# Hybrid decoder step on one core: the FFN's list of waiting pair work goes on across tiles, and sums of weights are made up to three units ahead

## The chip, the core and the metric

One Trainium2 chip, one core of it. The metric is device time in microseconds (us) of one launch. Engines: PE (TensorE, matrix products; PEld are its weight loads), DVE (VectorE), ACT (ScalarE), POOL (GpSimd), SP (SyncE, which here only issues loads).

## What is computed

A two-layer decoder trunk for 512 prompt tokens and 8 sample tokens, width 1024, float32. Each layer adds half a SwiGLU FFN, a mixing stage and another half FFN:

```python
def swiglu_ffn(x, wg, wu, wd):
    return (jax.nn.silu(x @ wg) * (x @ wu)) @ wd

x = x + 0.5 * swiglu_ffn(rms_norm(x, g1), wg1, wu1, wd1)
x = x + mix(rms_norm(x, gm))       # retention, sliding window attention, conv
x = x + 0.5 * swiglu_ffn(rms_norm(x, g2), wg2, wu2, wd2)
```

The FFN's hidden width is 2816. So there are four FFN blocks in the program, and the change lies in these alone.

## The kernel before

**Layout.** The activations x lie transposed: 8 blocks of 128 features by 520 columns (512 + 8), worked on as two halves of 260. Float32 products are made of a rounded high part and a low remainder of each factor. For each weight, ACT casts the high part (L290) and DVE subtracts to get the low part (L296); three matmuls then make one product (`mm3`, L342; `product`, L334).

**Weights.** They come in the order of use as 318 chunks of 128 x 1024 floats (512 KB) into a ring of four places, loaded by SP's queue (`load`, L238 to L245). A place is loaded anew when the last low split of its chunk is done. `ahead` (L303) is called at the start of each unit of weights: it issues the casts of units up to six slots ahead (a plain chunk is two slots, a product one), then the low splits, and then sums for coming units.

**Tiles.** A hidden tile is 128 of the 2816 hidden features: 22 tiles, numbered 0 to 21, each with a gate half (t) and an up half (u). The down projection runs in three steps: after tiles 0 to 8 step 0 uses tiles 0 to 7; after tiles 9 to 16 step 1 uses tiles 8 to 15; after tiles 17 to 21 step 2 uses the rest.

**Seven products.** The tiles 5, 6, 7, 9, 10, 11, 13, 14, 15, 17, 18, 20 and 21 ("paired") and down steps 0 and 1 take 2 x 2 block products with seven products instead of eight: a11, s1, s2, a12, s3, s4, a22 (`seven`, L523). s1, s2 and s4 need sums of weights, made by `sums` (L247) on DVE: s1 at L258, s2 at L260 and L261, s4 at L263. The chunk with a22 is released by a22's low split. In `seven`, ACT copies c11 to c22 (L528) ahead of product s2. On the side of the activations, sums of four blocks are needed too: `sum_parts` (L476) makes four sums on DVE (L461 to L464), two casts on ACT (L480) and two low splits on DVE (L484). `pair_blocks` (L499) puts three casts (L509) and three splits (L512) before it.

A plain tile (`hidden`, L439) has 16 weight tiles on PE, eight for the gate half and eight for the up half; after the first half DVE scales the gate half out of PE's result (L448), at the end the up half (L454).

**The list.** What follows a tile is put into a list of generators, `waiting`: first `gated` (L426), the gating u*silu(t) (L429 and L431 for paired tiles, silu at L434 on ACT, product L436 on DVE); then, for tiles with an odd number in groups 0 and 1, `pair_blocks`. `advance` (L412) does one step of the first generator in the list. It is called at every second weight tile of a plain tile and between the products of `seven`. `flush` (L420) does all that is left; `ffn` (L581) calls it at the end of each hidden tile, before the new work is put in, and at the start of each down step.

Each engine does its instructions in the order in which they are issued; where one waits, all behind it wait.

Of the kernel before, what the change touches and what calls it, by code (L numbers as in the profile page):

```python
# [23 lines left out]
PAIRED = (5, 6, 7, 9, 10, 11, 13, 14, 15, 17, 18, 20, 21)  # L24


GROUPS = ((0, 8, True), (8, 16, True), (16, 22, False))
# [91 lines left out]
def ffn_tiles(first, gate, up):  # L119


    return [(o, k) for k in range(KD) for o in (gate, up)] if first else [(o, k) for o in (gate, up) for k in range(KD)]
# [14 lines left out]
def step_kernel(ctx: ExitStack, tc: tile.TileContext, io: dict):  # L137
# [46 lines left out]
    def v2(t):  # L184
        return t.rearrange("p (a b) -> p a b", a=2)

    def unit(dt=F32):
        return units.tile([128, UNIT], dt, tag="m", name="m")
# [6 lines left out]
    def wt(name, n=NT, dt=F32, bufs=None):  # L195
        return work.tile([128, n], dt, tag="t", name=name)

    def ptile():
        return psum.tile([128, 2, 512], F32, tag="o", name="o")
# [4 lines left out]
    seq, slot = [], [0]  # L204
# [14 lines left out]
    chunk = [0]  # L219
# [16 lines left out]
    at, nxt, loaded, pending = [0, 0], [0], [0], []  # L236

    def load(dma=True):  # L238

        while loaded[0] < NCH and (loaded[0] < RAW or loaded[0] - RAW in done):  # L240
            i = loaded[0]
            loaded[0] += 1
            raw[i] = wraw.tile([128, CT * 128], F32, tag="w", name="w")
            if dma:
                nc.sync.dma_start(raw[i], io["w"][i])  # L245

    def sums(u):  # L247

        if u >= len(seq) or u in ready:
            return  # L250
        ready.add(u)
        name, i = seq[u]
        if name == "chunk":
            return
        load()
        (a21, a11), (a22, a12) = ((raw[j][:, :PC], raw[j][:, PC:]) for j in (i, i + 1))
        if name == "s1":
            nc.vector.tensor_add(Rd[:, 0, :PC], a21, a22)  # L258
        elif name == "s2":
            nc.vector.tensor_sub(a21, a21, a11)  # L260
            nc.vector.tensor_add(Rd[:, 1, :PC], a21, a22)  # L261
        elif name == "s4":
            nc.vector.tensor_sub(Rd[:, 0, :PC], a12, Rd[:, 1, :PC])  # L263
# [18 lines left out]
    def split_hi():  # L282

        u = nxt[0]
        if u < len(seq):
            nxt[0] += 1
            load()
            sums(u)
            spl[u] = parts_of(u)
            nc.scalar.copy(spl[u][0], source(u))  # L290
            pending.append(u)

    def split_lo(n=9):
        for u in pending[:n]:
            h, lo = spl[u]
            nc.vector.tensor_sub(lo, source(u), h.bitcast(F32))  # L296
            name, i = seq[u]
            if name in ("chunk", "s3", "a22"):
                done.add(i + (name == "a22"))
                load()  # L300
        del pending[:n]

    def ahead(u):  # L303

        old = len(pending)
        while nxt[0] < len(seq) and slot[nxt[0] + 1] - slot[u] <= 6:
            split_hi()
        if seq[u][0] == "chunk":
            split_lo()
        else:  # L310
            split_lo(old)
            sums(nxt[0])
            sums(nxt[0] + 1)

    def next_tile(look=True):
        u, c = at
        if c == 0 and look:
            ahead(u)
        at[:] = (u, c + 1) if c + 1 < CT else (u + 1, 0)
        s = slice(c * 128, (c + 1) * 128)  # L320
        return spl[u][0][:, s], spl[u][1][:, s]
# [17 lines left out]
    def mm3(o, w, vh, vl, first, last):  # L339
        for i, (a, b) in enumerate(((w[0], vl), (w[0], vh), (w[1], vh))):  # L340
            for s in range(2):
                nc.tensor.matmul(  # L342
                    o[:, s, :HN], lhsT=a, rhs=b[:, s * HN : (s + 1) * HN],
                    start=first and i == 0, stop=last and i == 2,
                )
# [20 lines left out]
    def run(parts):  # L366
        for _ in parts:
            pass
# [43 lines left out]
    waiting = []  # L412

    def advance():
        while waiting:
            try:
                next(waiting[0])
                return True
            except StopIteration:
                del waiting[0]  # L420

    def flush():
        while advance():
            pass
# [14 lines left out]
    def hidden(norm, first):  # L439

        og, ou = ptile(), ptile()
        for i, (o, k) in enumerate(ffn_tiles(first, og, ou)):
            mm3(o, next_tile(), xh[:, k], xl[:, k], k == 0, k == KD - 1)
            if i % 2:
                advance()
            if i + 1 == KD and not first:
                t = wt("t")
                nc.vector.tensor_mul(v2(t), og[:, :, :HN], v2(R))  # L448
        if first:
            run(norm)  # L450
            t = wt("t")
            nc.vector.tensor_mul(v2(t), og[:, :, :HN], v2(R))
        u = wt("u")
        nc.vector.tensor_mul(v2(u), ou[:, :, :HN], v2(R))  # L454
        return t, u, None

    def sums4(u, w):


        (b11, b12), (b21, b22) = ((z[:, :HN], z[:, HN:]) for z in (u, w))  # L460
        nc.vector.tensor_sub(b22, b12, b22)  # L461
        nc.vector.tensor_sub(b12, b12, b11)  # L462
        nc.vector.tensor_sub(b11, b11, b22)
        nc.vector.tensor_sub(b21, b21, b11)  # L464
        return u, w
# [4 lines left out]
    def meet(b, t):  # L470
        return {n: (b, t)[i][c] for n, (i, c) in MEET.items()}

    def halves(h, lo):
        return [tuple(z[:, i * HN : (i + 1) * HN] for z in (h, lo)) for i in range(4)]

    def sum_parts(th, tl, u, w):  # L476
        sums4(u, w)
        yield
        for i, src in enumerate((u, w)):
            nc.scalar.copy(th[:, i * NT : (i + 1) * NT], src)  # L480
        yield
        for i, src in enumerate((u, w)):
            c = slice(i * NT, (i + 1) * NT)
            nc.vector.tensor_sub(tl[:, c], src, th[:, c].bitcast(F32))  # L484
        yield
# [13 lines left out]
    def pair_blocks(u, w, spare, hs):  # L499

        if not spare:
            z = [unit(F32R) for _ in range(3)]
            spare += [z[i // 4][:, i % 4 * HN : (i % 4 + 1) * HN] for i in range(12)]
        th, tl = unit(F32R), unit(F32R)
        b = [(spare.pop(0), spare.pop(0)) for _ in range(3)]
        hs.append(meet(b, halves(th, tl)))
        src = u[:, :HN], w[:, :HN], w[:, HN:]
        for (h, _), a in zip(b, src):
            nc.scalar.copy(h, a)  # L509
        yield  # L510
        for (h, lo), a in zip(b, src):
            nc.vector.tensor_sub(lo, a, h.bitcast(F32))  # L512
        yield from sum_parts(th, tl, u, w)

    def two_parts(u, hs):
# [65 lines left out]
    def ffn(l, name, norm, after):  # L581
        hs, even, spare, xs = {n: [] for n in range(len(GROUPS))}, None, [], []
        for step, n in ffn_steps():
            if step == "hidden":
                g = next(i for i, (a, b, _) in enumerate(GROUPS) if a <= n < b)
                t, u, v = pair_hidden(xs) if n in PAIRED else hidden(norm, n == 0)
                flush()
                waiting.append(gated(t, u, v))
                if GROUPS[g][2] and n % 2:
                    waiting.append(pair_blocks(even, u, spare, hs[g]))  # L590
                elif GROUPS[g][2] or n == GROUPS[g][0]:
                    even = u
                else:
                    waiting.append(two_parts(u, hs[g]))
                waiting.extend(input_sums(l, name, j, xs) for j in {0: (0,), 1: (1, 2), 2: (3,)}.get(n, ()))
                continue
            flush()
            if GROUPS[n][2]:
                for m in range(0, KD, 2):
                    pair_down(m, hs[n])  # L600

                if not GROUPS[n + 1][2]:
                    waiting.append(two_parts(even, hs[n + 1]))
                continue
            if n == len(GROUPS) - 1 and name == "ffn1_norm":
                load_mix_constants()
            for m in range(KD):
                o = ptile()
                for f, h in enumerate(hs[n]):
                    mm3(o, next_tile(), *h, f == 0, f == len(hs[n]) - 1)  # L610
                nc.vector.scalar_tensor_tensor(
                    v2(x[:, m]), o[:, :, :HN], 0.5, v2(x[:, m]), op0=ALU.mult, op1=ALU.add
                )
                if n == len(GROUPS) - 1:
                    run(after(m))
# [818 lines left out]
```

## Time and profile before

| | us |
|---|---|
| three runs | 1906.8, 1906.71, 1905.59 |
| median | 1906.71 |
| the profiled execution | 1903.99 |
| its span | 1902.2 |
| its mean granted PE clock | 0.989 of full speed |

All times inside the prediction are of the profiled execution, counted from the start of its span. In rows of a timeline the columns are start, duration, engine, line, operation, out<-in and count; the bracket holds the idle time of the engine ahead of it and what ended it. Instructions of one line that follow each other are one row, with a count. Rows of waits give the total, how many times and the longest. Windows give the busy time of each engine in a stretch and PE's granted clock.

### The profile page before, as it was taken

What the parts mean: (1) busy time and instruction counts of PE and PEld (TensorE: products, weight loads), DVE (VectorE), ACT (ScalarE), POOL (GpSimd) and SP (SyncE); (2) the same over time, 40 slices, a digit from 0 to 9 for tenths busy, and PEclk for the clock granted to TensorE, in tenths of its full rate; (3) what the DMA queues carried; (4) which work ended last, traced back from release to release, by engine and by line L of the source; (5) the groups of instructions that cost most, each with busy time, mean ns of one, the idle gap of its engine ahead of it and who ended that gap; (6) DMA issues with size and microseconds to landing.
All of it is one profiled execution on the core that took longest, in us unless ns stands there. A gap on an engine that the chain in (4) does not pass through costs nothing.

```text
span 1902.2 us, 37220 instructions
## 1 busy us (share of the span) xinstructions
PE 1845.5 (97%) x15182; PEld 1821.8 (96%) x15182; DVE 1552.9 (82%) x2587; ACT 1051.3 (55%) x2052; POOL 23.3 (1%) x52
## 2 busy tenths in 40 slices
PE   8999999999999999999999999999998999999999
PEld 8999999999989999999999999999998999999999
DVE  8988888688667989888779888876886579889984
ACT  6655646533765656645555556565237556466452
POOL 0000000000100000000000000000000000000000
PEclk9999999999999999999999999999999999999999
DMA  5233224433312233323323232434333132333332
GB/s 182 79 100 112 90 89 127 129 104 115 117 43 92 78 90 100 102 88 107 116 80 100 87 92 89 124 114 125 101 113 105 45 100 68 95 108 100 92 96 90
DMA packets 54173, 189.37 MB, mean 100 GB/s; under 512 B 6273, under 2 KB 7153, under 8 KB 54001
## 3 DMA queue, kind: packets, MB, share of 16 engines
q1 hardware_dynamic: 50784, 177.35, 30.8%
q0 software_dynamic: 3072, 9.53, 1.5%
q8 instruction: 119, 1.95, 0.4%
q14 instruction: 54, 0.43, 0.1%
q10 hardware_dynamic: 144, 0.11, 0.0%
HBM read 179.50 MB, written 7.45 MB: 98 GB/s over the span
## 4 chain that ended last, share of the span: by engine, by line
PE 68%; DVE 20%; ACT 5%; issue 4%; DMA 3%; DVEq 0%; ACTq 0%; POOL 0%; POOLq 0%
PE o L342 37%; PE o L334 29%; DVE wl L296 4%; DVE wh L296 3%; DMA w<-in_w 2%; DVE m L484 2%; DVE u L436 1%; DVE m L512 1%; DVE u L431 1%; DVE w L260 1%; DVE t L431 1%; DVE t L429 1%; PE o L361 1%; ACT wh L290 1%; DVE u L462 1%
## 5 line engine op out<-in xcount | busy, mean ns | idle before, releaser
L342 PE MATMUL o<-xl,wh 128*128 128x260 f32 x1920 | 389.8, 284 | 6.5 <-DVE xl L387 6.0
L342 PE MATMUL o<-xh,wl 128*128 128x260 f32 x1920 | 387.6, 284 | 0.9 <-DVE wl L296 0.9
L342 PE MATMUL o<-xh,wh 128*128 128x260 f32 x1920 | 387.4, 283 | 0.0
L334 PE MATMUL o<-m,wh 128*128 128x260 f32 x2592 | 352.9, 286 | 16.8 <-ACT o L528 15.5
L290 ACT CAST wh<-w 128x1024 fp32r<-128x1024 f32 (+1 forms) x318 | 261.4, 822 | 193.3 <-PE o L342 134.9
L334 PE MATMUL o<-m,wl 128*128 128x260 f32 x2592 | 352.4, 285 | 16.2 <-ACT o L528 15.1
L334 PEld LDWEIGHTS o<-m,wh 128*128 128x128 f32 x2592 | 330.3, 191 | 20.9 <-ACT o L528 18.5
L334 PEld LDWEIGHTS o<-m,wl 128*128 128x128 f32 x2592 | 329.5, 190 | 20.0 <-ACT o L528 17.9
L342 PEld LDWEIGHTS o<-xl,wh 128*128 128x128 f32 x1920 | 297.4, 189 | 7.8 <-ACT wh L355 5.9
L342 PEld LDWEIGHTS o<-xh,wl 128*128 128x128 f32 x1920 | 297.1, 189 | 1.1 <-DVE wl L296 1.1
L342 PEld LDWEIGHTS o<-xh,wh 128*128 128x128 f32 x1920 | 296.6, 189 | 0.0
L296 DVE TENSOR_TENSOR wl<-w,wh 128x1024 fp32r<-128x1024 f32 x150 | 183.3, 1222 | 45.3 <-ACT wh L290 40.0
L342 PE MATMUL o<-m,wh 128*128 128x260 f32 x1024 | 164.5, 282 | 1.7 <-DVE m L520 1.7
L342 PEld LDWEIGHTS o<-m,wh 128*128 128x128 f32 x1024 | 140.0, 188 | 2.5 <-DVE m L520 2.5
L296 DVE TENSOR_TENSOR wh<-w,wh 128x512 fp32r<-128x512 f32 x168 | 115.1, 685 | 8.8 <-ACT wh L290 8.8
L296 DVE TENSOR_TENSOR wl<-w,wl 128x512 fp32r<-128x512 f32 x168 | 115.1, 685 | 8.7 <-ACT wl L290 8.7
L290 ACT CAST wl<-w 128x512 fp32r<-128x512 f32 x168 | 104.3, 621 | 30.0 <-PE o L334 16.1
L334 PE MATMUL o<-xh,wl 128*128 128x260 f32 x624 | 115.8, 283 | 0.0
L334 PE MATMUL o<-xh,wh 128*128 128x260 f32 x624 | 115.5, 282 | 0.0
L290 ACT CAST wl<-Rd 128x512 fp32r<-128x512 f32 x126 | 78.5, 623 | 59.6 <-PE o L334 27.8
L290 ACT CAST wh<-Rd 128x512 fp32r<-128x512 f32 x126 | 78.5, 623 | 57.5 <-PE o L334 26.3
L342 PE MATMUL o<-m,wl 128*128 128x260 f32 x512 | 102.7, 282 | 0.0
(219 smaller groups left out, 2674.7 us busy)
## 6 DMA issues: line engine op xcount, KB each, us to landing
w<-in_w SPq DMA_DIRECT2D x318, 512.0 KB, 3.6
out_y<-x SPq DMA_DIRECT2D x8, 260.0 KB, 2.0
m<-in_cm POOLq DMA_DIRECT2D x4, 512.0 KB, 4.2
m<-in_s_ret SPq DMA_DIRECT2D x4, 512.0 KB, 5.7
m<-sc POOLq DMA_DIRECT2D x8, 256.0 KB, 4.4
out_o_rets<-m POOLq DMA_DIRECT2D x4, 512.0 KB, 3.5
x<-in_x SPq DMA_DIRECT2D x3, 520.0 KB, 6.8
w<-in_w SPq DMA_DIRECT2D x4, 256.0 KB, 4.9
```

The costliest lines, as they stand in the source:

```text
L260: nc.vector.tensor_sub(a21, a21, a11)
L290: nc.scalar.copy(spl[u][0], source(u))
L296: nc.vector.tensor_sub(lo, source(u), h.bitcast(F32))
L334: nc.tensor.matmul(o, lhsT=a[:, s], rhs=b, start=first and j == 0 and i == 0, stop=j == JP - 1 and i == 2, skip_group_check=True,)
L342: nc.tensor.matmul(o[:, s, :HN], lhsT=a, rhs=b[:, s * HN : (s + 1) * HN], start=first and i == 0, stop=last and i == 2,)
L361: nc.tensor.matmul(o[:, s, :HN], lhsT=w, rhs=v[:, s * HN : (s + 1) * HN], start=i == 0, stop=i == len(parts) - 1,)
L429: nc.vector.tensor_add(d[:, HN:], d[:, HN:], v)
L431: nc.vector.tensor_mul(d, d, R)
L436: nc.vector.tensor_mul(u, u, t)
L462: nc.vector.tensor_sub(b12, b12, b11)
L484: nc.vector.tensor_sub(tl[:, c], src, th[:, c].bitcast(F32))
L512: nc.vector.tensor_sub(lo, a, h.bitcast(F32))
```

## The change

Four things change, all in the order in which the FFN's side work is issued.

1. `ahead` makes the sums of up to three coming units, where it made those of two. It stops at a unit whose chunks are not yet loading, and at an s1 while an s4 still waits for its low split.
2. `ffn` empties the list at the end of tiles 0 to 4 only. From tile 5 on the work of a tile stays in the list and goes on in the next tile, in order. At down steps 0 and 1 the list is emptied but for its last item, the gating of the plain tile just computed (8 or 16), which goes on in the down step.
3. `hidden` takes a step of the list at each weight tile, not only every second, while more than two items wait.
4. `sum_parts` gets an empty step behind its four sums, and `pair_blocks` one ahead of them: the same work in more steps.

```diff
@@ ahead
             split_lo(old)
-            sums(nxt[0])
-            sums(nxt[0] + 1)
+            for v in range(nxt[0], min(nxt[0] + 3, len(seq))):
+
+                load()
+                if seq[v][0] != "chunk" and seq[v][1] + 1 >= loaded[0]:
+                    break
+                if seq[v][0] == "s1" and any(seq[p][0] == "s4" for p in pending):
+                    break
+                sums(v)
@@ hidden
-            if i % 2:
+            if i % 2 or len(waiting) > 2:
                 advance()
@@ sum_parts
         sums4(u, w)
         yield
+        yield
         for i, src in enumerate((u, w)):
@@ pair_blocks
             nc.vector.tensor_sub(lo, a, h.bitcast(F32))
+        yield
         yield from sum_parts(th, tl, u, w)
@@ ffn
                 t, u, v = pair_hidden(xs) if n in PAIRED else hidden(norm, n == 0)
-                flush()
+                if n < PAIRED[0]:
+                    flush()
                 waiting.append(gated(t, u, v))
...
+            rest = [waiting.pop()] if GROUPS[n][2] else []
             flush()
+            waiting.extend(rest)
             if GROUPS[n][2]:
```

The same instructions are issued on each engine, and PE's order is the same; DVE's and ACT's orders differ. The lines of the new kernel lie 6 to 8 below those of the old (L436 is L442, L448 is L454, L454 is L460, L461 to L464 are L467 to L470, L484 is L491, L429 is L435, L431 is L437, L512 is L519); L258 to L296 keep their numbers.

Three places on DVE, in the first FFN block. First the passage from the last paired tile (7) to the plain tile 8, before:

```order
L484 TENSOR_TENSOR m<-u,m 128x520 x2
L296 TENSOR_TENSOR wh<-w,wh 128x512
L429 TENSOR_TENSOR t<-t,v 128x260
L429 TENSOR_TENSOR u<-u,v 128x260
L431 TENSOR_TENSOR t<-t,R 128x520
L431 TENSOR_TENSOR u<-u,R 128x520
L296 TENSOR_TENSOR wl<-Rd,wl 128x512
L296 TENSOR_TENSOR wh<-w,wh 128x512
L436 TENSOR_TENSOR u<-u,t 128x520
L296 TENSOR_TENSOR wl<-w,wh 128x1024
L258 TENSOR_TENSOR Rd<-w 128x512
```

The same place in the new kernel (an L296 of 128x512 is the low split of a product's weights, from Rd where these are a sum; one of 128x1024 that of a plain chunk):

```order
L296 TENSOR_TENSOR wl<-Rd,wl 128x512
L491 TENSOR_TENSOR m<-u,m 128x520 x2
L296 TENSOR_TENSOR wh<-w,wh 128x512
L435 TENSOR_TENSOR t<-t,v 128x260
L435 TENSOR_TENSOR u<-u,v 128x260
L437 TENSOR_TENSOR t<-t,R 128x520
L437 TENSOR_TENSOR u<-u,R 128x520
L258 TENSOR_TENSOR Rd<-w 128x512
L296 TENSOR_TENSOR wl<-w,wh 128x1024
L442 TENSOR_TENSOR u<-u,t 128x520
```

The four gating rows (L429 and L431, now L435 and L437) stand behind the two splits of s4 and a22, and the sum L258 of the next pair stands ahead of the plain chunk's split and of the product L436 (L442).

Next the start of down step 0 on DVE, from the last of the four sums to the sum s1 of the next unit, before:

```order
L464 TENSOR_TENSOR u<-u 128x260
L484 TENSOR_TENSOR m<-u,m 128x520 x2
L454 TENSOR_TENSOR u<-o,R 128x520
L436 TENSOR_TENSOR u<-u,t 128x520
L263 TENSOR_TENSOR Rd<-w,Rd 128x512
L296 TENSOR_TENSOR wl<-w,wl 128x512
L296 TENSOR_TENSOR wh<-Rd,wh 128x512
L258 TENSOR_TENSOR Rd<-w 128x512
```

The same place in the new kernel, down to the product of tile 8's gating:

```order
L470 TENSOR_TENSOR u<-u 128x260
L460 TENSOR_TENSOR u<-o,R 128x520
L491 TENSOR_TENSOR m<-u,m 128x520 x2
L263 TENSOR_TENSOR Rd<-w,Rd 128x512
L296 TENSOR_TENSOR wl<-w,wl 128x512
L296 TENSOR_TENSOR wh<-Rd,wh 128x512
L258 TENSOR_TENSOR Rd<-w 128x512
L260 TENSOR_TENSOR w<-w 128x512
L261 TENSOR_TENSOR Rd<-w 128x512
L442 TENSOR_TENSOR u<-u,t 128x520
```

The scaling L454 (L460) goes ahead of the splits of the activations, and the product L436 (L442) goes behind the sum s4 and the next sums.

Last, tile 4 on DVE, from the splits of three blocks to the sum s4, before:

```order
L512 TENSOR_TENSOR m<-u,m 128x260 x3
L461 TENSOR_TENSOR u<-u 128x260
L462 TENSOR_TENSOR u<-u 128x260
L463 TENSOR_TENSOR u<-u 128x260
L464 TENSOR_TENSOR u<-u 128x260
L448 TENSOR_TENSOR t<-o,R 128x520
L260 TENSOR_TENSOR w<-w 128x512
L261 TENSOR_TENSOR Rd<-w 128x512
L296 TENSOR_TENSOR wh<-Rd,wh 128x512
L296 TENSOR_TENSOR wl<-w,wl 128x512
L484 TENSOR_TENSOR m<-u,m 128x520 x2
L454 TENSOR_TENSOR u<-o,R 128x520
```

The same place in the new kernel:

```order
L519 TENSOR_TENSOR m<-u,m 128x260 x3
L454 TENSOR_TENSOR t<-o,R 128x520
L260 TENSOR_TENSOR w<-w 128x512
L261 TENSOR_TENSOR Rd<-w 128x512
L296 TENSOR_TENSOR wh<-Rd,wh 128x512
L296 TENSOR_TENSOR wl<-w,wl 128x512
L467 TENSOR_TENSOR u<-u 128x260
L468 TENSOR_TENSOR u<-u 128x260
L469 TENSOR_TENSOR u<-u 128x260
L470 TENSOR_TENSOR u<-u 128x260
L491 TENSOR_TENSOR m<-u,m 128x520 x2
L460 TENSOR_TENSOR u<-o,R 128x520
```

The four sums go behind the scaling of the gate half (L448, now L454), the sum s2 and two splits.

## The prediction

> **What bounds the kernel now.** I read the page's summary first, then the waits of the matmul engine, then those places engine by engine.
>
> ```profile
> PE 1845.5 (97%) x15182; PEld 1821.8 (96%) x15182; DVE 1552.9 (82%) x2587; ACT 1051.3 (55%) x2052; POOL 23.3 (1%) x52
> ```
>
> PE is busy 97% of the span, so the time can fall only where PE stands still. The waits of PE, longest total first (us in total, times, longest):
>
> ```profile
> PE o L334 <- ACT o L528: 30.6, 13, 3.0
> ```
>
> The copy L528 (c22 <- c11, ahead of product s2 of a seven-product tile) holds PE for 30.6 us. Twelve of the thirteen waits are long, three in each of the four FFN blocks: at the start of down step 0 (place 1), at hidden tile 13 (place 2) and at the start of down step 1 (place 3). These are the three of the first block, each stretch from the first product of the tile to the end of the wait (PE, PEld, DVE, ACT, POOL busy, granted clock, DMA share):
>
> ```profile
> 109.39:115.36 5.97, 3.04 (x26) 2.84 (x24) 5.45 (x11) 3.15 (x7) 0.00 (x0) 1.00 0.01 3
> 195.36:200.59 5.23, 3.05 (x26) 2.84 (x24) 4.76 (x10) 2.62 (x6) 0.00 (x0) 1.00 0.00 0
> 240.22:246.30 6.08, 3.15 (x27) 2.87 (x25) 5.56 (x11) 3.15 (x7) 0.00 (x0) 1.00 0.01 3
> ```
>
> DVE is busy for nine tenths of each stretch while PE does 3.0 us of work in 5.2 to 6.1: DVE ends last here. Place 1 on PE, ACT and DVE, in time:
>
> ```profile
> 115.36 0.39 PE L334 MATMUL o<-m,wl 128*128 128x260 f32 x1 [2.93 <-ACT o L528]
> ...
> 114.42 0.62 ACT L290 CAST wh<-Rd 128x512 fp32r<-128x512 f32 x1 [1.82 <-DVE Rd L263]
> 114.94 0.37 ACT L528 COPY o<-o 128x260 f32<-128x260 f32 x1
> ...
> 110.40 0.43 DVE L464 TENSOR_TENSOR u<-u 128x260 f32<-128x260 f32 x1
> 111.05 1.31 DVE L484 TENSOR_TENSOR m<-u,m 128x520 fp32r<-128x520 f32 x2 [0.23 <-ACT m L480]
> 112.28 0.69 DVE L454 TENSOR_TENSOR u<-o,R 128x520 f32<-128x520 f32 x1
> 113.08 0.70 DVE L436 TENSOR_TENSOR u<-u,t 128x520 f32<-128x520 f32 x1
> 113.70 0.68 DVE L263 TENSOR_TENSOR Rd<-w,Rd 128x512 f32<-128x512 f32 x1
> ```
>
> PE waits for L528; on ACT's queue L528 stands behind the cast of the sum s4, which waits for L263; on DVE's queue L263 stands behind L484, L454 and L436, none of which it needs. Place 2 has the same shape, without L436 ahead of the sum:
>
> ```profile
> 197.04 1.31 DVE L484 TENSOR_TENSOR m<-u,m 128x520 fp32r<-128x520 f32 x2 [0.23 <-ACT m L480]
> 198.27 0.69 DVE L454 TENSOR_TENSOR u<-o,R 128x520 f32<-128x520 f32 x1
> 198.88 0.68 DVE L263 TENSOR_TENSOR Rd<-w,Rd 128x512 f32<-128x512 f32 x1
> ```
>
> Why DVE comes late to place 1 is seen one tile earlier on DVE, at the passage from the last seven-product tile (7) to the plain tile 8:
>
> ```profile
> 91.09 0.42 DVE L429 TENSOR_TENSOR t<-t,v 128x260 f32<-128x260 f32 x1
> ...
> 93.00 0.68 DVE L296 TENSOR_TENSOR wl<-Rd,wl 128x512 fp32r<-128x512 f32 x1
> 93.60 0.69 DVE L296 TENSOR_TENSOR wh<-w,wh 128x512 fp32r<-128x512 f32 x1
> 94.20 0.69 DVE L436 TENSOR_TENSOR u<-u,t 128x520 f32<-128x520 f32 x1
> 94.81 1.22 DVE L296 TENSOR_TENSOR wl<-w,wh 128x1024 fp32r<-128x1024 f32 x1
> 98.23 0.69 DVE L258 TENSOR_TENSOR Rd<-w 128x512 f32<-128x512 f32 x1 [2.20 <-DMA w<-in_w]
> 98.84 1.22 DVE L296 TENSOR_TENSOR wl<-w,wh 128x1024 fp32r<-128x1024 f32 x1
> 99.97 0.69 DVE L260 TENSOR_TENSOR w<-w 128x512 f32<-128x512 f32 x1
> ```
>
> ```profile
> 94.31 3.80 DMA w<-in_w
> ```
>
> The split at 93.60 is the last use of a raw chunk (a22); the load into that place takes 3.80 us; L258, the next pair's sum s1, waits 2.20 us for it; and from there to L263 at 113.70 the chain of waits names DVE, with short casts of ACT between, and never PE. In all, DVE waits for loads at L258:
>
> ```profile
> DVE Rd L258 <- DMA w<-in_w: 20.8, 10, 2.3
> ```
>
> So the end of place 1 is set by the a22 split one tile earlier, plus the load, plus the row of DVE work behind it.
>
> **The change, part by part.** It adds and removes no instruction; PE's order stays. Only DVE and ACT rows move. All lines below are those of the kernel before.
>
> *At tiles 7, 11 and 15 the gating goes behind the splits.* The list is no longer emptied at the tile's end, so L429 twice and L431 twice now stand behind the splits of s4 and a22: from 91.09 to 93.00, 1.91 us of DVE work. The a22 split, and with it the load, can start up to x = 1.91 us earlier. Lower bound x = 0 (the split waits for something else). The load may also take longer, as it starts closer to the one before. Two loads 2 us apart:
>
> ```profile
> L245 SPq DMA_DIRECT2D w<-in_w x2: 327/328/328, 124.4 to 126.4; - x2
> ...
> DMA to landing us min/median/max: 3.6/4.0/4.5
> ```
>
> Against 3.80 that is up to 0.7 more. Here the load before is the one that the s3 split releases: 3.1 us earlier now (91.09 to 94.20, the rows behind each split), 2.4 us then, since one split and two L484 still lie between and the gating doesn't (0.6 + 1.2 + 0.6, an estimate from the spacings above). That is a third of the way from 3.1 to 2.0, so I take 0.2 of the 0.7: x = 1.7.
>
> *L258 goes ahead of plain work.* Looking three units ahead puts L258 in front of tile 8's first split (94.81; the next such one, 98.84 to 99.97, holds DVE 1.13) and of L436 (94.20 to 94.81, 0.61), which filled the time until the landing. So 1.74 us that lay beside the load now lies behind it. DVE's wait at L258 hardly shrinks, and tile 8's first split comes late for PE. I price that second effect at nothing: the split would end at 98.23 - 1.7 + 0.61 + 1.22 = 98.4 and not at 96.0, so PE loses at most 2.3 us there, even if it used the split at once; place 1 ends by DVE's row, 2.93 us behind PE, and what PE loses in tile 8 it waits less at place 1. If DVE were not last there, it would cost up to 2.3 us a place, 28 in all.
>
> [...]
>
> *At places 1 and 3* L436 goes behind L263, and L454 goes ahead of L484, where it fills the idle 0.23. L436 costs 113.70 - 113.08 = 0.62, the gap ahead of it 113.08 - 112.28 = 0.80 less the usual 0.61 (198.88 - 198.27), 0.19; with the 0.23 that is 1.04 less ahead of L263. *At place 2* L263 goes ahead of the two L484: 198.27 - 197.04 = 1.23, and the 0.23 ahead of them, 1.46.
>
> So L528 comes earlier, at places 1 and 3 by x - 1.74 + 1.04 = x - 0.70, at place 2 by x - 1.74 + 1.46 = x - 0.28. A block gains 3x - 1.68; with x = 1.7 that is 3.42, four blocks 13.7. The places add up, since DVE waits for PE again between them. No place has its wait used up: 1.0 of 2.9 at places 1 and 3, 1.4 of some 2.2 at place 2.
>
> *A loss at tile 4 to 5.* The extra step in the list puts the four sums L461 to L464 behind L448, L260, L261 and two splits. L448 needs the first half of tile 4 on PE. Second block, DVE, ACT, PE:
>
> ```profile
> 640.52 0.43 DVE L461 TENSOR_TENSOR u<-u 128x260 f32<-128x260 f32 x1
> ...
> 642.26 0.69 DVE L448 TENSOR_TENSOR t<-o,R 128x520 f32<-128x520 f32 x1
> ...
> 646.23 1.30 DVE L484 TENSOR_TENSOR m<-u,m 128x520 fp32r<-128x520 f32 x2
> ...
> 648.06 0.68 DVE L263 TENSOR_TENSOR Rd<-w,Rd 128x512 f32<-128x512 f32 x1
> ...
> 649.35 0.37 ACT L528 COPY o<-o 128x260 f32<-128x260 f32 x1
> ...
> 641.16 0.40 PE L342 MATMUL o<-xl,wh 128*128 128x260 f32 x2
> ...
> 649.80 1.44 PE L334 MATMUL o<-m,wl 128*128 128x260 f32 x10
> ```
>
> Today the L461 group fills DVE's time until PE is at its half (641.16). Now L448 stands there and waits, as it does in another tile, for the half plus 0.19 us (311.51 - 311.32):
>
> ```profile
> 311.51 0.70 DVE L448 TENSOR_TENSOR t<-o,R 128x520 f32<-128x520 f32 x1 [0.62 <-PE o L342]
> ...
> 311.32 0.40 PE L342 MATMUL o<-xl,wh 128*128 128x260 f32 x2
> ```
>
> L448 then starts at 641.16 + 0.19 = 641.35, not 642.26, and DVE is idle for 0.8 us ahead of it. The rows behind come 0.91 earlier, up to L484's old slot (646.23 - 0.91 = 645.32). There the four sums stand now: three spacings of 0.47 and, from L464 to L484 through the casts L480, 0.65 (111.05 - 110.40), 2.05 in all. L484 comes at 647.37, 1.14 later, and with it L263 and L528. L528 ended at 649.72 and PE was ready at 649.80: a new wait of 1.06 us in blocks two to four. In the first block PE waits there already, and by the same walk L263 moves by 0.78: 0.8 more.
>
> ```profile
> 69.74 1.71 PE L334 MATMUL o<-m,wh 128*128 128x260 f32 x12 [0.17 <-ACT o L528]
> ```
>
> Sum 3 x 1.06 + 0.8 = 4.0. Bounds: 0 (the first half of tile 4 is done earlier against DVE than in this run) and 4 x 1.14 + the 0.4 that a further wait for the casts adds, 5.
>
> *The rest* (the list running on in tiles 5 to 7, 9 to 11, 13 to 15 and 17 to 21; the last gating kept for the down step, where DVE has its own slack beside four tiles of products) I cost at nothing: PE shows no wait there. Cover gone, it would be L436's 0.6 us a place.
>
> **Sum.** 1903.99 (span 1902.2 and 1.8 around it) - 13.7 + 4.0 = 1894.3. The median of the three runs, 1906.71, lies 2.7 above the profiled run; the same is added: **1897.0**. Own range: x = 1.91 without the loss gives -16.2, 1890.5; x = 1.2 (the landing's whole 0.7 lost) with it gives -3.7, 1903.
>
> **Rivals.**
> - *The waits at L528 vanish* (DVE gets ahead for good, as its idle time before L258 is used): -30.6 + 4.0, 1880 (1876 without the loss, 1889 if a third of them stays). For: 10 waits of DVE there are 20.8 us. Against: L258 still waits for its load. Chance 0.12.
> - *No change.* The load is slower by what it starts earlier, and x stays near 0.89, at which 12x - 6.7 only pays the 4.0: 1903 to 1910, that is x from 1.2 to 0.6. For: the 4.5 us landing, 0.7 over 3.80; a pause of DVE ahead of the a22 split that takes another 0.3. Chance 0.12.
> - *Slower: the landing gates plain work.* If the a22 split is not earlier (x = 0: its cast on ACT or the products release it, not DVE's row), L258 with its wait stands in front of tile 8's split for nothing. Places 1 and 3 lose 0.70, place 2 0.28: 4 x 1.68 + 4.0 = +10.7, 1917. It decides below x = 0.89. Worse, a wait of 2.93 + 0.70 = 3.6 us nears the one after which PE's clock falls. After a wait of 4.63 us in the mixing stage it was halved:
>
> ```profile
> 522.85:527.48 4.63, 0.00 (x1) 0.00 (x1) 3.82 (x8) 4.50 (x9) 0.00 (x0) 0.92 0.00 0
> 527.48:531.00 3.52, 3.52 (x16) 2.68 (x17) 3.45 (x7) 3.46 (x8) 0.00 (x0) 0.50 0.02 5
> ```
>
> Half speed for 3.52 us loses 1.8 us a time, at eight places 14 more: 1917 to 1932. Against: DVE's rows from 91.09 to 94.20 stand back to back, so DVE's row does hold the split, as far as the rows show. Chance 0.12.
>
> [...]
>
> **How the numbers follow.** Forecast 0.64, the three rivals 0.12 each. No change can be told within 0.2%, 3.8 us: 1902.9 to 1910.5. The forecast's own range and the first rival lie below that, the second rival within, the third above: 0.76, 0.12, 0.12. The range takes the forecast whole, most of the no-change case and the upper half of the bigger gain: 1884 to 1908, leaving out the slower case and half of the first rival, 0.18.
>
> **What would show it.** Right: the waits for L528 still twelve long ones, places 1 and 3 near 1.9 and place 2 near 0.8 us, some 22 in all with the new ones (30.6 - 13.7 + 4.0 = 20.9); L258's DVE wait near 2.2 at the last paired tile, now ahead of the plain tile's split; a short PE wait for that split; a new wait of about 1 us for L528 in tile 5. Wrong: long waits gone or as long as before; a22's split at tile 7 not earlier against PE; the clock below 1.00 behind place 1 or 3; a long PE wait inside a down step, where I priced the kept gating at nothing.

## The result and the profile after

| | before | after |
|---|---|---|
| median, us | 1906.76 (1905.59 to 1913.0) | 1889.13 (1888.96 to 1890.91) |
| profiled execution, us | 1903.99 | 1888.96 |
| its span | 1902.2 | 1886.9 |
| its PE busy time | 1845.5 | 1835.9 |
| its mean granted clock | 0.989 | 0.995 |

The ratio is 0.9912, with an interval of 0.9896 to 0.9929: 17.6 us faster, where the prediction said 9.7 (1906.71 to 1897.0) with a range of 1884 to 1908. The direction and the range hold; more than half of the size comes from where the prediction had put nothing, PE's clock. The page after, then the waits of PE (L536 is the copy L528 of before):

```profile
PE 1835.9 (97%) x15182; PEld 1812.8 (96%) x15182; DVE 1558.1 (83%) x2587; ACT 1050.7 (56%) x2052; POOL 23.3 (1%) x52
```

```profile
PE o L340 <- ACT o L536: 18.1, 16, 1.6
PE o L348 <- DVE wl L296: 8.8, 13, 1.6
```

The waits for the copy fell by 12.5 us, from 30.6; waits for the plain tile's split rose by 7.9, of which 7.2 are twelve new waits at tiles 8, 12 and 16 (the one wait of before, 0.9, lies in the mixing stage). PE's time outside its busy time is 1902.2 - 1845.5 = 56.7 before and 1886.9 - 1835.9 = 51.0 after, 5.7 less. The other 9.6 of the span's 15.3 us are busy time, with the same 15182 matmuls: PE ran faster. The clock shows it. The first 3.4 us behind each long wait before (PE, PEld, DVE, ACT, POOL busy, granted clock, DMA share, GB/s):

```profile
115.36:118.76 3.40, 3.40 (x28) 3.40 (x29) 3.33 (x6) 2.08 (x5) 0.00 (x0) 1.00 0.57 170
...
246.30:249.70 3.40, 3.40 (x18) 3.40 (x19) 3.33 (x6) 1.86 (x4) 0.00 (x0) 0.58 0.69 180
...
825.73:829.13 3.40, 3.40 (x21) 3.40 (x22) 3.33 (x6) 1.91 (x4) 0.00 (x0) 0.71 0.65 171
1058.03:1061.43 3.40, 3.40 (x20) 3.40 (x21) 3.33 (x6) 1.91 (x4) 0.00 (x0) 0.68 0.67 180
1144.40:1147.80 3.40, 3.40 (x16) 3.40 (x17) 3.33 (x6) 2.29 (x6) 0.00 (x0) 0.53 0.61 165
1191.55:1194.95 3.40, 3.40 (x18) 3.40 (x19) 3.33 (x6) 1.90 (x4) 0.00 (x0) 0.62 0.66 186
1641.70:1645.10 3.40, 3.40 (x20) 3.40 (x21) 3.33 (x6) 1.91 (x4) 0.00 (x0) 0.68 0.63 178
```

Behind six of the twelve waits PE ran for part of the time at half speed, 16 to 21 matmuls in 3.40 us instead of 28. Six times 3.40 us times what is missing to 1.00 (2.20 in sum) is 7.5 us lost inside these windows. The half-speed stretches run on past them: in the trace's record of the clock each of the six lasts 3.41 us at 0.50, so six lose up to 10.2 us, which covers the 9.6. After the change all twelve windows show 1.00, such as these:

```profile
114.84:118.24 3.40, 3.40 (x28) 3.40 (x29) 3.30 (x6) 2.61 (x6) 0.00 (x0) 1.00 0.52 154
...
1133.55:1136.95 3.40, 3.40 (x28) 3.40 (x29) 3.30 (x6) 2.77 (x6) 0.00 (x0) 1.00 0.49 130
```

Now the passage from tile 7 to tile 8 on DVE (L437 is L431, L442 is L436), with PE's first matmuls of tile 8:

```profile
92.54 0.69 DVE L296 TENSOR_TENSOR wh<-w,wh 128x512 fp32r<-128x512 f32 x1
...
94.43 0.69 DVE L437 TENSOR_TENSOR u<-u,R 128x520 f32<-128x520 f32 x1
97.08 0.69 DVE L258 TENSOR_TENSOR Rd<-w 128x512 f32<-128x512 f32 x1 [1.96 <-DMA w<-in_w]
97.69 1.22 DVE L296 TENSOR_TENSOR wl<-w,wh 128x1024 fp32r<-128x1024 f32 x1
98.83 0.69 DVE L442 TENSOR_TENSOR u<-u,t 128x520 f32<-128x520 f32 x1
...
97.90 0.40 PE L348 MATMUL o<-xl,wh 128*128 128x260 f32 x2
...
98.97 0.51 PE L348 MATMUL o<-xh,wl 128*128 128x260 f32 x2 [0.43 <-DVE wl L296]
```

The a22 split starts 1.06 us earlier (93.60 to 92.54), not 1.91, counted from the start of the span, in which PE has lost 0.8 us more by then, in tile 5; L258 still waits about 2 us; the plain split and L442 stand behind it, and PE waits for that split. The rest of place 1:

```profile
113.18 0.68 DVE L263 TENSOR_TENSOR Rd<-w,Rd 128x512 f32<-128x512 f32 x1
...
114.84 0.63 PE L340 MATMUL o<-m,wl 128*128 128x260 f32 x3 [1.52 <-ACT o L536]
```

From L258 to L263 it is 16.10 us here, against 15.47 before (98.23 to 113.70): 0.63 more, where the prediction had 1.74 - 1.04 = 0.70. And the forecast loss at tile 4 to 5 is there. L454 (L448 of before) waits for PE in tile 4, and PE waits for the copy in tile 5:

```profile
60.89 0.70 DVE L454 TENSOR_TENSOR t<-o,R 128x520 f32<-128x520 f32 x1 [0.96 <-PE o L348]
...
70.47 0.74 PE L340 MATMUL o<-m,wh 128*128 128x260 f32 x4 [0.97 <-ACT o L536]
```

### The profile page after: what moved, and what is told of

Same layout as the page of the kernel before. It is cut to its first block, busy times and chain, and to the rows that moved or that the text cites. A ratio compares the mean times of both kernels' runs of the same rounds, so it can differ in the third digit from the quotient of the medians.

```text
span 1886.9 us, 37178 instructions
## 1 busy us (share of the span) xinstructions
PE 1835.9 (97%) x15182; PEld 1812.8 (96%) x15182; DVE 1558.1 (83%) x2587; ACT 1050.7 (56%) x2052; POOL 23.3 (1%) x52
## 4 chain that ended last, share of the span: by engine, by line
PE 77%; DVE 14%; ACT 5%; DMA 2%; issue 2%; DVEq 0%; ACTq 0%; POOL 0%; POOLq 0%
PE o L348 38%; PE o L340 37%; DVE wl L296 3%; DMA w<-in_w 2%; DVE wh L296 2%; DVE m L491 1%; DVE u L442 1%; DVE m L519 1%; PE o L367 1%; ACT wh L290 1%; DVE t L437 1%; ACT t L440 1%; DVE w L260 1%; ACT wl L290 0%; DVE Rd L263 0%
## 5 line engine op out<-in xcount | busy, mean ns | idle before, releaser
L340 PE MATMUL o<-m,wh 128*128 128x260 f32 x2592 | 347.7, 283 | 9.2 <-ACT o L536 9.2
L340 PE MATMUL o<-m,wl 128*128 128x260 f32 x2592 | 347.8, 283 | 8.9 <-ACT o L536 8.9
L340 PEld LDWEIGHTS o<-m,wh 128*128 128x128 f32 x2592 | 325.7, 188 | 11.7 <-ACT o L536 10.9
L296 DVE TENSOR_TENSOR wl<-w,wh 128x1024 fp32r<-128x1024 f32 x150 | 183.2, 1221 | 38.0 <-ACT wh L290 33.3
L348 PE MATMUL o<-m,wh 128*128 128x260 f32 x1024 | 164.5, 282 | 1.7 <-DVE m L528 1.7
L296 DVE TENSOR_TENSOR wl<-w,wl 128x512 fp32r<-128x512 f32 x168 | 115.0, 685 | 6.3 <-ACT wl L290 6.1
L296 DVE TENSOR_TENSOR wh<-w,wh 128x512 fp32r<-128x512 f32 x168 | 115.0, 685 | 6.2 <-ACT wh L290 6.1
L440 ACT ACTIVATE t<-t 128x520 f32<-128x520 f32 x88 | 56.1, 638 | 94.0 <-DVE t L437 93.7
L290 ACT CAST wh<-Rd 128x512 fp32r<-128x512 f32 x126 | 78.6, 624 | 45.3 <-PE o L340 17.3
```

Source lines behind the costliest of these rows:

```text
L340: nc.tensor.matmul(o, lhsT=a[:, s], rhs=b, start=first and j == 0 and i == 0, stop=j == JP - 1 and i == 2, skip_group_check=True,)
L348: nc.tensor.matmul(o[:, s, :HN], lhsT=a, rhs=b[:, s * HN : (s + 1) * HN], start=first and i == 0, stop=last and i == 2,)
L440: nc.scalar.activation(t, t, AF.Silu)
```

## The experiments

**Theory A:** the list across tiles, with its empty steps, brings the gain, because it puts the a22 split and so the load ahead of the gating; the third unit of sums costs 1.74 us a place. **Rival B:** the third unit brings the gain. **Theory C:** half of the measured gain is PE's clock. **Rival D:** the clock's difference belongs to the single run. The kernel before, beside these runs, took 1904.30 us (e1 to e4), 1905.02 (e5 to e8) and 1903.65 (e9, e10). The changed kernel's 1889.13 us stood beside 1906.76 of the kernel before, so a difference between a run below and the changed kernel holds to about 2 to 3 us.

**e1, the third unit undone.**

```diff
-            for v in range(nxt[0], min(nxt[0] + 3, len(seq))):
+            for v in range(nxt[0], min(nxt[0] + 2, len(seq))):
```

> The changed kernel, but sums of weights only two units ahead, as before; the list still goes on across tiles. On DVE at tiles 8, 12 and 16 the plain tile's first split (1.13 us) and the gating's product (0.61) stand ahead of the sum s1 (L258) again, where they fill its wait for the load (1.7 to 2.5 us in the changed kernel's trace). Theory A (the list across tiles brings the gain, the third unit of sums costs 1.74 us a place): waits for the split at the plain tile gone, the sum s4 1.74 us earlier against PE at all twelve places, the two kinds of PE wait there, together 21.5 us in the changed kernel, fall to about 3.4; time about 1871, between 1866 and 1877. Theory B (the third unit of sums brings the gain): about as before the change where it counts, 1889 or more.

Measured: 1865.07 us (1863.12 to 1867.61), ratio to before 0.9787 (0.977 to 0.9803), 24 us below the changed kernel. DVE at the passage, DVE's waits for loads at L258, and PE's waits:

```profile
94.71 1.22 DVE L296 TENSOR_TENSOR wl<-w,wh 128x1024 fp32r<-128x1024 f32 x1
95.85 0.69 DVE L442 TENSOR_TENSOR u<-u,t 128x520 f32<-128x520 f32 x1
96.83 0.69 DVE L258 TENSOR_TENSOR Rd<-w 128x512 f32<-128x512 f32 x1 [0.29 <-DMA w<-in_w]
```

```profile
DVE Rd L258 <- DMA w<-in_w: 3.9, 6, 1.4
```

```profile
PE o L340 <- ACT o L536: 10.8, 12, 1.5
PE o L348 <- DVE wl L296: 0.7, 1, 0.7
```

The 1.74 us of work now fill the wait for the load, which almost disappears. The split is waited for at no plain tile (the one wait left is in the mixing stage). A holds, B falls: the third unit is a loss of 24 us that the rest of the change covered. It is 6 us more than A had: PE's busy time falls from 1835.9 to 1828.9 us, though both traces hold about the same time at half speed (granted clock 0.995 and 0.994). That is 0.16 to 0.28 us at each split and each copy where the wait shrinks or goes; why is not shown.

**e2, the list emptied at each tile.**

```diff
-                if n < PAIRED[0]:
-                    flush()
+                flush()
```

> The changed kernel, but the list is emptied at the end of each hidden tile, as before; sums still three units ahead. The gating at tiles 7, 11 and 15 stands ahead of the splits of s4 and a22 again, so the load for s1 is not earlier, and s1 with its wait stands ahead of the plain tile's first split. Theory A (list brings, third unit costs): about 0.9 us later at each of twelve places than in the changed kernel, 10 us: 1899, and up to 1908 if PE's clock falls after the longer waits; longer PE waits for the plain tile's split (over 1 us each). Theory B (the third unit brings the gain): 1889 or less.

Measured: 1902.49 us (1900.45 to 1905.66), ratio 0.999 (0.9979 to 1.0).

```profile
PE o L348 <- DVE wl L296: 17.8, 13, 1.9
```

With the gating ahead of the a22 split again the load is late, and PE waits more than twice as long for the plain split. 13 us over the changed kernel, as A has it. Much of it, 10.9 us of PE's time, is lost in tiles 7, 11 and 15 themselves, where short breaks of PE come back (see x below).

**e3, no empty steps.** Both of the added `yield` lines are taken out.

```diff
         sums4(u, w)
         yield
-        yield
...
-        yield
         yield from sum_parts(th, tl, u, w)
```

> The changed kernel without the two empty steps in the activation sums. Without them the list runs two steps earlier: the wait of about 1 us at tile 5 should go (four times, 3.7 us), but the gating at tiles 7, 11 and 15 comes ahead of the splits of s4 and a22 again, so the load for s1 is not earlier. Theory A: -3.7 + 10 + 3.7 (small waits at the copies of the last paired tile come back) = about +10, 1899. Rival: the empty steps only cost, and without them it is 1885.

Measured: 1904.09 us (1899.75 to 1907.12), ratio 0.9996 (0.9984 to 1.0008): A, by 5 us more than expected. PE loses 14.0 us in tiles 7, 11 and 15, which A had at 3.7. DVE at the passage:

```profile
92.10 0.69 DVE L437 TENSOR_TENSOR u<-u,R 128x520 f32<-128x520 f32 x1
92.71 0.68 DVE L296 TENSOR_TENSOR wl<-Rd,wl 128x512 fp32r<-128x512 f32 x1
93.31 0.68 DVE L296 TENSOR_TENSOR wh<-w,wh 128x512 fp32r<-128x512 f32 x1
...
97.92 0.69 DVE L258 TENSOR_TENSOR Rd<-w 128x512 f32<-128x512 f32 x1 [3.31 <-DMA w<-in_w]
```

The gating (L437) stands ahead of the two splits again. It is the empty steps that hold it back behind them; a list that merely goes on does not.

**e4 and e7, longer waits at the same order.** L460 (L454 of before) is done three times (e4) or twice (e7) at tiles 8, 12 and 16.

```diff
-        nc.vector.tensor_mul(v2(u), ou[:, :, :HN], v2(R))
+        for _ in range(1 + again):
+            nc.vector.tensor_mul(v2(u), ou[:, :, :HN], v2(R))
...
-                t, u, v = pair_hidden(xs) if n in PAIRED else hidden(norm, n == 0)
+                t, u, v = pair_hidden(xs) if n in PAIRED else hidden(norm, n == 0, 2 if n in (8, 12, 16) else 0)
```

> The changed kernel with the scaling of the up half (L460) done three times instead of once at tiles 8, 12 and 16: the same values again, 2 x 0.61 us more on DVE ahead of the sum s4 at the twelve places. This brings the waits for L536 there from 1.5 and 0.5 us to 2.7 and 1.7, near those of before the change. Theory C (about half of the measured gain is PE's clock, which falls to half behind some of the waits of 1.9 us and more, and behind none of 1.6): more than the 12 x 1.22 = 14.6 us that the waits give by themselves, by 4 to 10 us: 1908 to 1914, and windows behind the waits with a granted clock of 0.5 to 0.7 in some of the twelve. Rival D (the clock's difference is a matter of the single run): 1889 + 14.6 = 1904, clock 1.00 behind all twelve.

> As e4_longer_waits, with one repetition instead of two: 12 x 0.61 = 7.3 us by the waits alone, which become about 2.1 and 1.1 us. 1896.5 if PE's clock does not fall behind waits of 2.1; 1900 to 1904 if it does in about half of the eight, as behind the 2.0 us waits of e4_longer_waits; half of the windows behind the waits then show a clock under 0.8.

Measured: e4 1917.39 us (1914.67 to 1921.14), 28 over the changed kernel for 14.6 of added work; e7 1901.6 (1898.62 to 1903.86), 12.5 over for 7.3. Places 2 and 3 of block one and place 3 of block three in e4, behind the wait:

```profile
203.14:206.54 3.40, 3.40 (x28) 3.40 (x29) 3.30 (x6) 2.77 (x6) 0.00 (x0) 1.00 0.46 122
250.19:253.59 3.40, 3.40 (x15) 3.40 (x16) 3.30 (x6) 1.94 (x5) 0.00 (x0) 0.50 0.51 154
...
1201.65:1205.05 3.40, 3.40 (x19) 3.40 (x20) 3.30 (x6) 2.44 (x5) 0.00 (x0) 0.63 0.51 154
```

Nine of e4's twelve windows lie between 0.50 and 0.65, which loses 13.7 us by the same sum as above. PE's busy time is 1850.2, 14.3 over the changed kernel's. The waits grew too. They are now two in a row at places 1 and 3, at L492 (L484) and at the copy:

```profile
PE o L340 <- ACT o L537: 24.0, 16, 2.0
PE o L340 <- DVE m L492: 11.0, 8, 1.4
```

That is 35.0 for 18.1. So 16.9 us of wait and 14 of clock, less 0.6 at the plain splits, come near the span's 29.6. In e7 three of twelve windows are low, such as this one:

```profile
694.71:698.11 3.40, 3.40 (x16) 3.40 (x17) 3.30 (x6) 1.94 (x5) 0.00 (x0) 0.51 0.54 157
```

C holds and D falls: put the waits back, and the clock falls again (0.986 granted in e4 and 0.992 in e7, 0.995 in the changed kernel). e7 was expected to show it at half of the eight; it showed it at three.

**e5, the empty steps only from tile 5 on, with two units.**

```diff
-    def sum_parts(th, tl, u, w):
+    def sum_parts(th, tl, u, w, more=False):
         sums4(u, w)
         yield
-        yield
+        if more:
+            yield
...
-                    waiting.append(pair_blocks(even, u, spare, hs[g]))
+                    waiting.append(pair_blocks(even, u, spare, hs[g], n >= PAIRED[0]))
```

> The kernel of e1_two_units (sums two units ahead, list across tiles), with the empty steps only in the pair work that starts at tile 5 or later, so that the activation sums at tile 4 stand ahead of the scaling of the gate half (L448) again. If the wait at tile 5 for L528 (0.97 to 0.98 us in blocks two to four, 0.8 more in the first) comes from that move alone, it goes, 3.7 us: 1861, between 1859 and 1863. Rival: something else holds L528 there (the casts ahead of it on ACT), the wait stays: 1865.

Measured: 1861.28 us (1858.34 to 1864.4), ratio to before 0.9776 (0.9754 to 0.9798). The waits for the copy:

```profile
PE o L340 <- ACT o L538: 6.4, 8, 1.5
```

The four waits at tile 5 are gone, eight remain, all at places 1 and 3. This is the best kernel of the study: 44 us below before, 28 below the changed one, with the list across tiles, its steps where they help, and sums two units ahead.

**e6, no gating kept for the down step.**

```diff
-            rest = [waiting.pop()] if GROUPS[n][2] else []
+            rest = []
```

> The changed kernel, but the list is emptied whole at down steps 0 and 1: the gating's product of tile 8 and 16 stands ahead of the sum s4 again. Theory: 0.62 + 0.19 us a place at eight places, 6.5 us: 1895.5; up to 1902 if PE's clock falls behind some of the waits, which become 2.3 us. Rival: the kept gating gets in the way in the down step and gives back what it saves: 1889 or less.

Measured: 1900.35 us (1897.54 to 1904.36), ratio 0.9978 (0.9963 to 0.9993). The copy's waits:

```profile
PE o L340 <- ACT o L536: 22.9, 16, 2.2
```

They are 4.8 us more; PE's busy time is 1841.9, 6.0 more, at a granted clock of 0.991 for 0.995. So the kept gating is worth 11 us, half of it clock.

**e8, the third unit alone on the kernel before.**

```diff
-            sums(nxt[0])
-            sums(nxt[0] + 1)
+            for v in range(nxt[0], min(nxt[0] + 3, len(seq))):
...
+                sums(v)
```

> The kernel before with one part of the change alone: sums up to three units ahead. The sum s1 with its wait for the load stands ahead of the plain tile's first split (1.13 us), the load is not earlier. Theory A: 1.13 us a place at twelve places, 13.6 us: 1918, up to 1925 with the clock. Theory B (the third unit brings the gain): under 1904.

Measured: 1916.96 us (1912.02 to 1918.48), ratio 1.0065 (1.0045 to 1.0086): 12 us slower, near the 13.6 of A. B falls a second time. The nearness is partly luck. Without the time that half speed cost, PE takes 17.3 us more over the four FFN blocks in this trace: 18.3 more at the plain split, 5.1 more in the last paired tiles, 6.2 less at the copy. And its clock fell once in these blocks, not six times, which gave up to 8.5 us back (0.994 granted over the span, 0.989 before).

**e9, list and kept gating without the steps, two units.** The edits of e1 and e3 together.

> The changed kernel without the two empty steps and with sums two units ahead: what is left is the list that goes on across tiles and the gating kept for the down step. At tiles 7, 11 and 15 the order on DVE is then that of the kernel before (gating ahead of the splits of s4 and a22, the plain split ahead of s1); only the gating's product goes behind the sum s4 at places 1 and 3. Theory A (the list alone does not move the a22 split; it takes the empty steps for that): 8 x 0.81 = 6.5 us less than before, and up to 4 us of clock: 1894 to 1899. Rival: the list across tiles is what brings the a22 split forward, with or without the steps: 1861 to 1870.

Measured: 1889.87 us (1887.8 to 1897.09), ratio 0.9931 (0.9906 to 0.9957). It lies between the two ranges, 4 us below A's. The waits say that only A's clock term was off:

```profile
PE o L340 <- ACT o L534: 23.7, 12, 2.1
```

The waits fell by 6.9 from 30.6, close to the 6.5. The rest is clock: PE is busy 1835.6 us, 9.9 less than before, with one half-speed stretch in the FFN blocks for six (0.995 granted, 0.989 before). With waits of 2.0 us on average and 2.1 at most at the twelve places one window is low (the first) and eleven are full:

```profile
114.50:117.90 3.40, 3.40 (x15) 3.40 (x16) 3.34 (x6) 1.94 (x5) 0.00 (x0) 0.50 0.56 160
201.13:204.53 3.40, 3.40 (x28) 3.40 (x29) 3.33 (x6) 2.69 (x6) 0.00 (x0) 1.00 0.59 159
```

**e10, a step of the list at every second weight tile only.**

```diff
-            if i % 2 or len(waiting) > 2:
+            if i % 2:
```

> The changed kernel, but a plain tile takes a step of the list at every second weight tile only. The rows move at tiles 1 and 2 alone, where PE has no wait: same as the changed kernel, 1889 within 3 us. Rival: it delays tile 3 or 4: 1 us or more a block, 1893 and up.

Measured: 1898.72 us (1896.27 to 1904.76), ratio 0.9974 (0.9959 to 0.9989): 9.6 us slower than the changed kernel. The expectation was wrong and its rival right. In tile 2 the scaling L454 now stands one split earlier on DVE and waits for PE. In tile 4 it no longer waits but comes late, and PE's wait in tile 5 is three times as long:

```profile
37.51 0.70 DVE L454 TENSOR_TENSOR t<-o,R 128x520 f32<-128x520 f32 x1 [1.84 <-PE o L348]
...
62.65 0.69 DVE L454 TENSOR_TENSOR t<-o,R 128x520 f32<-128x520 f32 x1
...
72.22 0.63 PE L340 MATMUL o<-m,wh 128*128 128x260 f32 x3 [3.04 <-ACT o L536]
```

DVE's order differs in tile 2 alone, but DVE has not made up the 1.84 us that it stands there when tile 5 comes. The clock fell behind three of the four waits at tile 5, now 2.7 to 3.0 us long; over the span 0.993 was granted, 0.995 in the changed kernel.

## Why the prediction held, and where it did not

**The place.** Right: DVE's row from L258 to L263 ends last, and its order sets the wait. That row is 0.62 us longer at places 1 and 3 and 0.20 at place 2 (forecast 0.70 and 0.28). The copy still has twelve waits there, 1.5 us at places 1 and 3 and 0.5 at place 2; the text said 1.9 and 0.8, without what PE now waits for the plain split instead.

**x, the earlier load.** Right, if it is measured from a mark that the change does not move. PE's order is the same in both kernels, so the same matmul can be found in both traces. Against the matmuls of the last paired tile, the a22 split ends 1.66 us earlier on average (1.40 to 1.97 over the twelve passages), and L258 starts 1.59 earlier (1.12 to 2.03), where the prediction took 1.7. Its step on the load holds a slip: 2.4 lies two thirds of the way from 3.1 to 2.0, not a third, which would make x 1.5; the trace gives back only 0.07 between split and L258. With the measured values its formula gives 12 x 1.59 - 8 x 0.62 - 4 x 0.20 = 13.3 us, for 13.7.

Against the first matmul of tile 8, 12 or 16 the same rows are only 0.93 and 0.86 us earlier. The difference is PE: it gets there 0.73 us earlier itself. In tile 7 before, PE breaks off twice for a moment: product s2 waits for the copy L528, and product s3 for L535, the copy c12 <- c22 behind s2. The weight loads (PEld) show them as waits; the twelve at L535 are gone after the change:

```profile
PEld o L334 <- ACT o L535: 4.3, 12, 0.6
```

The start of products s1 and s3 of tile 7, before and after:

```profile
88.54 1.60 PE L334 MATMUL o<-m,wl 128*128 128x260 f32 x12
...
93.47 1.70 PE L334 MATMUL o<-m,wh 128*128 128x260 f32 x12
...
89.27 1.60 PE L340 MATMUL o<-m,wl 128*128 128x260 f32 x12
...
93.60 1.60 PE L340 MATMUL o<-m,wh 128*128 128x260 f32 x12
```

From the one to the other it takes 4.33 us instead of 4.93. So part of the gain shows in tile 7 and not at place 1. What PE's time between the same matmuls did over the four blocks, with the loss at half speed taken out:

| | us | forecast |
|---|---|---|
| tiles 7, 11, 15 | -8.7 | |
| the plain split at tiles 8, 12, 16 | +10.4 | |
| the copy at places 1, 2, 3 | -13.7 | |
| these three together | -12.0 | -13.7 |
| tile 5 | +4.2 | +4.0 |
| the rest of the blocks | +0.8 | 0 |
| **sum** | **-7.0** | **-9.7** |

Outside the blocks 1.6 us are lost, most of them in the second mixing stage, for a reason that no run here shows. So waits and breaks together give 5.4 of the span's 15.3 us.

**The plain split.** Right that PE waits for it (0.15 to 1.17 us at each of the twelve), and that this costs nothing beside the copy's wait, which shrinks by as much.

**The loss at tile 5.** Right: 0.80, 0.98, 0.97 and 0.97, 3.7 us for 4.0. e5 shows the cause.

**"I cost at nothing".** The kept gating was in the sum (0.81 a place) and was worth 4.8 us of wait. The step at each weight tile was not in the sum; without it 9.6 us are lost, so the loss at tile 5 would have been three times the forecast. The running on in the paired tiles, where the prediction saw no wait of PE, is where the short breaks of tiles 7, 11 and 15 went; by the sum above it is the same gain seen earlier, not one on top.

**The clock.** The step that failed. That "the time can fall only where PE stands still" left out PE's own speed: its busy time fell by 9.6 us. The text feared for the clock only behind waits of 3.6 us. Its windows of places 1 to 3 show 1.00, but they end where the wait ends; the stretch that matters begins there. Six of the twelve waits had been followed by half speed, one of them a wait of only 1.88 us (1144.40). Each such stretch is 3.41 us long at 0.50 and so costs up to 1.7 us. So the waits and breaks gave 5.4 us and the clock 9.8 in the profiled runs. That the range held owes nothing to the clock, for which it had no term; that 17.6 came out as far above 9.7 as it did is due to it.

Which waits were followed by half speed can be read from the traces. In those of before and after every half-speed stretch that ends before the span does lasts 3.41 us or twice that, and in either trace the starts lie whole multiples of 3.41 us apart (before, in the FFN blocks: 246.88, 827.14, 1059.25, 1144.58, 1192.37 and 1642.93; after, in the mixing stages alone: 485.23, 522.78, 1420.49 and 1461.45). So the starts of a trace lie on one grid with cells of 3.41 us. The cells around two waits of the kernel before, the one at 115.36 (2.93 us) and the one at 1144.40 (1.88 us):

```profile
110.34:113.75 3.41, 2.09 (x18) 1.89 (x16) 3.04 (x7) 2.20 (x4) 0.00 (x0) 1.00 0.02 5
113.75:117.16 3.41, 1.80 (x15) 1.80 (x16) 3.29 (x7) 2.01 (x5) 0.00 (x0) 1.00 0.30 80
117.17:120.58 3.41, 3.41 (x31) 3.41 (x30) 3.38 (x6) 2.04 (x5) 0.00 (x0) 1.00 0.65 221
...
1141.17:1144.58 3.41, 1.53 (x13) 1.32 (x12) 3.27 (x6) 1.82 (x5) 0.00 (x0) 1.00 0.00 0
1144.58:1147.99 3.41, 3.41 (x17) 3.41 (x17) 3.34 (x7) 2.30 (x6) 0.00 (x0) 0.50 0.67 172
```

The longer wait is cut in two by the grid, and PE works for more than half of either cell (2.09 and 1.80 us); the shorter lies whole in one, with 1.53 us of work. In the FFN blocks of before, half speed began behind six cells, in which PE had been busy for 0.58 to 1.53 us. In those of all twelve traces it began behind 30 cells, with PE busy for 0.58 to 1.68 us in 29 of them and for 1.90 in one (e5, 235.34). Of the other cells there (from 12 us into the span on, where the record of the clock begins), none had PE busy for less than 1.54; between that and 1.68 it went either way. In the mixing stages of before it also began behind two cells in which PE was busy throughout (3.41 us at 485.81 and at 1431.30), so PE's busy time alone does not tell it there. The waits of the changed kernel, 1.57 us at most at the copy, leave 1.85 us of work or more in each cell, and none of the twelve was followed by half speed. Counted back to the start of the span, the grid begins at 1.12 us before and at 0.54 after. The 23 executions of the kernel before beside e5 to e8 range from 1899.23 us (clock 0.991) to 1911.21 us (0.985); that it is the place of the grid that changes from one to the next, and with it how many waits of 2 to 3 us fall whole into a cell, is the author's estimate.

**Waiting early.** The third unit put L258's wait ahead of ready work. e1 prices it at 24 us in the changed kernel, e8 at 12 in the old one (19.7 and 17.3 of PE's time in the FFN blocks without half speed). The prediction had the term, 1.74 us a place, but took the change as one piece and did not work out what it would be without.

## What to carry to other kernels

Price a wait of the matmul engine with the granted clock that the trace shows behind it, not of the wait itself: here it was 0.53 to 0.71 in the 3.40 us behind six of twelve waits, and the change that brought the twelve from 1.71 to 2.98 us down to 1.57 at most gave 9.8 us in clock for 5.4 in waits and breaks. Put ready work ahead of the instruction that waits for a load: after the change the plain split (97.69) stood on DVE behind L258, which waited 1.96 us for its load, and in e8, with that order on the kernel before, PE's waits for such splits came to 15.8 us, where they had been 0.9. Take each part of a change that moves such work on its own: here one part gave 40 us and another took 24 back. Measure how much earlier a row comes against a mark that the change does not move: a short break that goes ahead of the mark hides a part of the gain.

## What was not expected of the hardware

PE's clock fell to half behind waits of 1.88 to 2.98 us in six of twelve cases before and stayed at 1.00 behind the other six, of 1.71 to 2.93 us. It fell behind two waits of about 1.4 and 1.5 us in a row in all eight of e4's (0.50 to 0.65 in the 3.40 us behind them), and behind none of the twelve of the changed kernel (at most 1.57 at the copy). Waits of 2.0 us on average had it in one of twelve in e9 (0.50). Length alone does not tell them apart: 1.88 us (1144.40) was followed by half speed, 1.87 (780.19) and 2.93 (115.36) were not. In the grid of 3.41 us the first lies whole in one cell, which has 1.53 us of work; the other two are cut by it. Why e5's cell with 1.90 us of work was followed by half speed, and the two cells of 3.41 us of work in the mixing stages, stays open.
